# Seven products instead of eight for the down-projection of three SwiGLUs

## The chip, the cores and the metric

The kernel runs on one core of a Trainium2 chip. The metric is the device time of one execution in microseconds (us). A core has five engines with a queue of instructions each, worked off in order: TensorE (PE: products of matrices, with the weight loads PEld beside them), VectorE (DVE), ScalarE (ACT), GpSimd (POOL) and SyncE (SP), which here only issues transfers. POOL also issues transfers, among them those that add to what stands at the destination. The engines work at the same time and wait for one another by semaphores.

## The reference

The reference is a decoder trunk of two layers on 512 tokens of 1024 float32 features. Each layer is SwiGLU, mixer (windowed attention and a short convolution side by side), SwiGLU:

```
x = x + 0.5 * swiglu(rms_norm(x), wg, wu, wd)     # SwiGLU 1 and 3
x = x + concat([attention, conv]) @ w_out         # mixer
x = x + 0.5 * swiglu(rms_norm(x), wg, wu, wd)     # SwiGLU 2 and 4
swiglu(h) = (silu(h @ wg) * (h @ wu)) @ wd        # wg, wu: 1024 x 2816, wd: 2816 x 1024
```

A last norm ends it. The change concerns `@ wd` in SwiGLUs 2, 3 and 4.

## The kernel before

The kernel keeps float32 accuracy with the faster fp32r products: each operand is split into a high part (a cast on ScalarE, line 190) and a low part (a subtraction on VectorE, line 191), and a product is the sum of three parts, high by high, high by low and low by high. So each tile of weight costs a load, a cast, a subtraction, and then its products.

x lies transposed in eight tiles `xs` of 128 features by 512 tokens. The 2816 inner features of a SwiGLU are 11 blocks of 256. A list of stages orders the work: `FIRST` for SwiGLU 1, `INNER` for 2 and 3, `LAST` for 4. ("p", b) is the up-projection of one block in plain form, ("w", b) that of the two blocks b and b+1, and ("d", blocks) the down-projection of these blocks, in which `down` yields 8 output chunks and line 810 adds half of each to x.

A ("w", b) stage (`winograd2`, products at line 725) computes gate and up with seven products of quarter matrices instead of eight, after Winograd's form of Strassen's method. `CHAINS` lists the seven: the accumulator (x, y or w in PSUM), the operand made from the normed activations (b11, b21, t2, t3, t1, t4, b22), and whether it starts anew. The weight quarters a11, a12, s2, s3, s1, a22, s4 come from `FORMS`. `up2` plans their transfers in two halves h each: s1 and s3 are sums that a second, accumulating transfer from POOL makes in the buffer (line 185), s2 and s4 are sums on VectorE (lines 208 and 234). The operands are made by `Norm.make` ahead of use, from the normed activations in `full`.

The weight tiles go through three stations. `need_raw` issues loads on SP into 8 buffers `raw`, `need_split` makes high and low parts into 3 buffers each (`wh`, `wl`), two tiles ahead of the products, and `take_split` hands them over. The activations of a w stage are transposed on TensorE (line 771, `turn`), split and stored as high and low parts in buffers of `g4` (8 of them). `flush` runs the pending transposes within the stages that follow. In the last SwiGLU, `Finale` (lines 827 to 945) computes the last four block pairs with tokens on the partitions, adds x, norms and stores.

The program is recorded line by line, and a scheduler then sets the order on each engine by data and buffers; the semaphores follow from that order.

Of the kernel before, what the change touches and what calls it, by code (L numbers as in the profile page):

```python
# [15 lines left out]
P = 128  # L16
# [13 lines left out]

FIRST = (
# [24 lines left out]
def trunk_kernel(  # L56
# [38 lines left out]
    def g4(name, dt=F32R, shape=(P, 2, S)):  # L95
        return work.tile(list(shape), dt, tag="g4", bufs=8, name=name)
# [96 lines left out]
    def need_split(g):  # L193
        while state["split"] <= min(g, len(order) - 1):
# [6 lines left out]
            elif isinstance(what, tuple):  # L201

                what, h, far = what
                last = {"a11": 0, "a12": 4, "s2": 2, "s3": 6, "s1": 2, "a22": 8, "s4": 4}[what]
                need_raw(u + max(last, 4) + h + LOAD_AHEAD)
                a11, s1, a12, s3, a22 = (raw_of.get(u + 2 * i + h) for i in range(5))
                if what == "s2":
                    nc.vector.tensor_add(a11, a11, s1)
                raw = {"a11": a11, "a12": a12, "s2": a11, "s3": s3, "s1": s1, "a22": a22, "s4": a12}[what]
            else:  # L210

                need_raw(u + 4 + LOAD_AHEAD)
                a11, a12, s1, s3, a22 = (raw_of.get(u + i) for i in range(5))
                if what == "s2":
                    nc.vector.tensor_add(a11, a11, s1)
                if what == "s4":
                    nc.vector.tensor_add(a11, a11, a12)
                raw = {"a11": a11, "a12": a12, "s2": a11, "s3": s3, "s1": s1, "a22": a22, "s4": a11}[what]
                if what == FORMS[-1]:
                    for i in range(5):  # L220
                        del raw_of[u + i]
# [60 lines left out]
    def plan():  # L282
# [20 lines left out]
        def up2(wg, wu, b, far):  # L303
            def at(w, half, h):
                return w, KC // 2 * half + 2 * h, 2, 2 * b * P, S

            u = len(units)
            for what in (
                ((wg, 0),), ((wu, 0), (wu, 1)), ((wg, 1),), ((wu, 0), (wg, 0)), ((wu, 1),)
            ):  # L310
                for h in range(2):
                    add_unit(*(at(w, half, h) for w, half in what))
            order.extend(
                (u, (what, h, far and what == "a11" and h == 0)) for what in FORMS for h in range(2)
            )

        def ffn(wg, wu, wd, stages):
            for what, b in stages:
# [5 lines left out]
                if what == "w":  # L324
                    up2(wg, wu, b, b == 1)
# [24 lines left out]
    xs = [xpool.tile([P, S], F32, tag=f"x{c}", name=f"x{c}") for c in range(KC)]  # L350
# [10 lines left out]
    class Norm:  # L361
# [60 lines left out]
        def scale(self, room):  # L422

            self.full = [g4(f"hf_{self.i}_{n}", F32, (P, 2, S)) for n in range(KC // 2)]
            for c in range(KC):
                nc.vector.scalar_tensor_tensor(
                    self.full[c // 2][:, c % 2, :],
# [6 lines left out]
            self.forms = {}  # L434
            self.sums = [room(f"sum{n}_{self.i}", F32, (P, KC // 2, H)) for n in range(2)]

        def make(self, *names):


            for what in names:  # L440
                hi, lo = (form(f"f{what}{n}_{self.i}") for n in "hl")
                self.forms[what] = (hi, lo)
                for q in range(2):
                    at = slice(2 * q, 2 * q + 2)
                    b11, b12, b21, b22 = (
                        self.full[2 * j + q][:, :, t * H : (t + 1) * H]
                        for j in range(2)
                        for t in range(2)
                    )
                    t3, t2 = (t[:, at, :] for t in self.sums)  # L450
                    if what == "t2":
                        nc.vector.tensor_sub(t3, b12, b22)
                        nc.vector.tensor_sub(t2, t3, b11)
                    if what == "t1":
                        nc.vector.tensor_sub(b12, b11, b12)
                    if what == "t4":
                        nc.vector.tensor_add(t2, t2, b21)
                    src = {"b11": b11, "b21": b21, "b22": b22, "t1": b12, "t3": t3}.get(what, t2)
                    split(hi[:, at, :], lo[:, at, :], src)
# [6 lines left out]
    xin = [g4(f"xin_{n}", F32) for n in range(4)]  # L466
# [130 lines left out]
    def ffn(norm, stages, after=None, late=None):  # L597
# [4 lines left out]
        def plain(b):  # L602
# [9 lines left out]
            hi, lo = g4(f"ah_{norm.i}_{b}"), g4(f"al_{norm.i}_{b}")  # L612
# [6 lines left out]
            if norm.inv is None:  # L619
# [3 lines left out]
                norm.scale(stock if first else g4)  # L623
# [17 lines left out]
        def winograd(b):  # L641
# [10 lines left out]
            hi, lo = g4(f"ah_{name}"), g4(f"al_{name}")  # L652
# [44 lines left out]
        def winograd2(b, between=None):  # L697
# [12 lines left out]
            for step, (acc, operand, start) in enumerate(CHAINS):  # L710
                if operand not in norm.forms:
                    norm.make(operand)
# [44 lines left out]
                if step == 2:  # L757
                    flush(2, "mm")
                if between:
                    between(step)  # L760
                if not first and step < 3:
                    ahead = CHAINS[step + 4][1]
                    if ahead not in norm.forms:
                        norm.make(ahead)
            for j in range(2):
                acts[b + j] = (g4(f"ah_{name}_{j}"), g4(f"al_{name}_{j}"))

            def turn(c, tag="sc"):
                tp = psum(tag, [P, S], f"at_{name}_{c}")
                for t in range(NT):  # L770
                    nc.tensor.transpose(  # L771
                        tp[:, t * P : (t + 1) * P], ups[t][:, c * P : (c + 1) * P], ident
                    )
                hi, lo = acts[b + c // 2]
# [3 lines left out]

        pending = []
# [6 lines left out]
        end = None  # L786
        for i, (what, b) in enumerate(stages):
            if what == "w":
                if after is None and b == 9:
                    end = Finale()  # L790
                winograd2(b, end and end.step)
# [10 lines left out]
            if final and end:  # L802
                end.down(b, acts, flush)
# [17 lines left out]
    class Finale:  # L821
# [8 lines left out]
        def step(self, n):  # L830

            for at in (0, 1) if n == 0 else (n + 1,):
                t, half = divmod(at, 2)
                if half == 0:
                    self.y.append(form(f"ytok{t}", F32, (P, D)))
                tp = psum("mm", [P, S], f"yt_{t}_{half}")
                for j in range(NT):
                    nc.tensor.transpose(
                        tp[:, j * P : (j + 1) * P],
                        xs[half * NT + j][:, t * P : (t + 1) * P],  # L840
                        ident,
                    )
                nc.scalar.copy(self.y[t][:, half * S : (half + 1) * S], tp)

        def widen(self, half, i, pairs):
            if half == 0:
                _, hi, lo = take_split()
            else:
                u = len(units) - pairs + i
                need_raw(u)  # L850
                hi, lo = (form(f"ww{n}_{i}", shape=(P, 2, S)) for n in "hl")
                split(hi, lo, raw_of.pop(u))
            self.w[half].extend((hi[:, k, :], lo[:, k, :]) for k in range(2))

        def products(self, acc, rhs, half, t, c0, a, b):

            tok = slice(t * P, (t + 1) * P)
            cols = slice(c0, c0 + acc.shape[1])
            for k in range(a, b):
                ah, al = rhs[k]  # L860
# [3 lines left out]
                nc.tensor.matmul(  # L864
                    acc, al[:, tok], wh[:, cols], start=False, stop=k + 1 == self.blocks
                )
# [19 lines left out]
        def down(self, blocks, acts, flush):  # L886
# [7 lines left out]
            pairs = len(blocks)  # L894
            self.blocks = 2 * pairs
            rhs = []

            def take(blocks):
                rhs.extend((acts[k][0][:, j, :], acts[k][1][:, j, :]) for k in blocks for j in range(2))


            ready = blocks[:-2]
            take(ready)
            for i in range(len(ready)):
                self.widen(0, i, pairs)
            accs = [psum("mm", [P, S], f"end_0_{t}") for t in range(NT)]
            for t in range(NT):
                self.products(accs[t], rhs, 0, t, 0, 0, len(rhs))
                flush()
            take(blocks[-2:])  # L910
            for i in range(len(ready), pairs):
                self.widen(0, i, pairs)
            for t in range(NT):
                rest = done[:, t : t + 1]
                self.products(accs[t], rhs, 0, t, 0, 2 * len(ready), len(rhs))
                self.close(accs[t], 0, t, 0, rest)
                nc.vector.tensor_scalar(rest, rest, 1.0 / D, EPS, op0=ALU.mult, op1=ALU.add)
                if t == 0:
                    for i in range(pairs):
                        self.widen(1, i, pairs)  # L920
            for t in range(NT):
# [4 lines left out]
                for i in range(steps):  # L926
                    ssq = small(f"ssq_end{t}_{i}", 1)
                    acc = psum("mm", [P, wide], f"end_1_{t}_{i}")
                    self.products(acc, rhs, 1, t, i * wide, 0, len(rhs))
# [18 lines left out]
    def mix(l, norm, after):  # L948
# [23 lines left out]
        for g in range(NKV):  # L972
            h = g4(f"mh_{l}_{g}"), g4(f"ml_{l}_{g}")
# [124 lines left out]
        for pair in range(2):  # L1098
# [21 lines left out]
            hi, lo = g4(f"mh_{l}_{2 + pair}"), g4(f"ml_{l}_{2 + pair}")  # L1120
# [59 lines left out]
```

## Time and profile before

| | |
|---|---|
| three runs | 1723.38, 1723.80, 1723.99 us; median 1723.8 |
| profiled execution | 1723.67 us, span 1721.9 us from the first to the last instruction |
| busy: TensorE, weight loads, VectorE, ScalarE, POOL | 1713.1, 1418.3, 1229.7, 844.2, 156.6 us |
| granted clock of TensorE | 1.0 |
| moved by DMA | 237.85 MB, 138 GB/s in the mean |

The page of the profile gives busy times for each engine, and groups instructions by line and tile. The chain of waits follows the work back from the last instruction, each step to what released it; shares of that chain say which engine sets the time. A row of a timeline or of the chain in order of time has the start, the length in us, the engine, the line and the operation; "x24" merges 24 equal neighbours. The view of stretches gives the busy time of each engine in a part of the span. The end of a matmul is modelled, so successive starts are the better measure of its cost.

### The profile page before, as it was taken

What the parts mean: (1) busy time and instruction counts of PE and PEld (TensorE: products, weight loads), DVE (VectorE), ACT (ScalarE), POOL (GpSimd) and SP (SyncE); (2) the same over time, 40 slices, a digit from 0 to 9 for tenths busy, and PEclk for the clock granted to TensorE, in tenths of its full rate; (3) what the DMA queues carried; (4) which work ended last, traced back from release to release, by engine and by line L of the source; (5) the groups of instructions that cost most, each with busy time, mean ns of one, the idle gap of its engine ahead of it and who ended that gap; (6) DMA issues with size and microseconds to landing.
All of it is one profiled execution on the core that took longest, in us unless ns stands there. A gap on an engine that the chain in (4) does not pass through costs nothing.

```text
span 1721.9 us, 20808 instructions
## 1 busy us (share of the span) xinstructions
PE 1713.1 (99%) x7922; PEld 1418.3 (82%) x7922; DVE 1229.7 (71%) x1694; ACT 844.2 (49%) x1227; POOL 156.6 (9%) x142
## 2 busy tenths in 40 slices
PE   9999999999999999999999999999999999999998
PEld 7888888988888888888888888888888888888887
DVE  7986666678858866766698666666787598666763
ACT  6544444456545544444465444444565465354353
POOL 1011000001201110110011100100022011100101
PEclk9999999999999999999999999999999999999999
DMA  8467455421337674574366745743124458664541
GB/s 245 107 164 208 132 135 150 128 78 58 105 108 146 172 199 131 135 195 132 102 147 179 203 131 136 184 145 99 51 62 123 117 115 221 159 178 125 138 135 49
DMA packets 201207, 237.85 MB, mean 138 GB/s; under 512 B 7628, under 2 KB 125460, under 8 KB 201108
## 3 DMA queue, kind: packets, MB, share of 16 engines
q1 hardware_dynamic: 176932, 189.46, 35.9%
q0 software_dynamic: 23024, 45.62, 16.0%
q8 instruction: 62, 1.02, 0.2%
q10 hardware_dynamic: 1152, 1.45, 0.2%
q14 instruction: 37, 0.30, 0.1%
HBM read 229.68 MB, written 2.10 MB: 135 GB/s over the span
## 4 chain that ended last, share of the span: by engine, by line
PE 97%; DVE 2%; ACT 1%; issue 0%; ACTq 0%; DVEq 0%
PE x L725 24%; PE acc L256 15%; PE acc L259 15%; PE acc L263 15%; PE y L725 12%; PE w L725 6%; PE at L771 2%; PE end L864 1%; PE end L862 1%; PE end L863 1%; PE x L669 1%; PE pt L1048 1%; DVE p L1041 0%; DVE wl L191 0%; ACT p L1033 0%; PE y L669 0%
## 5 line engine op out<-in xcount | busy, mean ns | idle before, releaser
L190 ACT CAST wh<-raw 128x1024 fp32r<-128x1024 f32 (+2 forms) x424 | 443.0, 1045 | 616.1 <-PE acc L259 243.1
L191 DVE TENSOR_TENSOR wl<-raw,wh 128x1024 fp32r<-128x1024 f32 (+2 forms) x423 | 518.5, 1227 | 232.7 <-ACT wh L190 231.5
L256 PE MATMUL acc<-ah,wh 128*128 128x512 f32 x640 | 254.4, 399 | 0.2 <-ACT ah L190 0.2
L263 PE MATMUL acc<-ah,wl 128*128 128x512 f32 x640 | 250.0, 391 | 0.0
L259 PE MATMUL acc<-al,wh 128*128 128x512 f32 x640 | 249.1, 389 | 0.0
L810 DVE SCALAR_TENSOR_TENSOR x<-acc,x 128x512 f32<-128x512 f32 x176 | 119.8, 689 | 107.0 <-PE acc L263 106.4
L256 PE MATMUL acc<-xh,wh 128*128 128x512 f32 x448 | 176.6, 394 | 0.1
L259 PE MATMUL acc<-xl,wh 128*128 128x512 f32 x448 | 175.2, 391 | 0.1
L263 PE MATMUL acc<-xh,wl 128*128 128x512 f32 x416 | 162.4, 390 | 0.0
L263 PEld LDWEIGHTS acc<-ah,wl 128*128 128x128 f32 x640 | 120.1, 188 | 26.0
L256 PEld LDWEIGHTS acc<-ah,wh 128*128 128x128 f32 x640 | 120.0, 188 | 24.0 <-ACT ah L190 1.4
L259 PEld LDWEIGHTS acc<-al,wh 128*128 128x128 f32 x640 | 120.4, 188 | 23.3
L185 POOL DMA_DIRECT2D raw<-in_ffn_wu_dram x39 | 47.2, 1211 | 807.9 <-DVE u L749 394.0
L259 PEld LDWEIGHTS acc<-xl,wh 128*128 128x128 f32 x448 | 84.2, 188 | 18.1 <-DVE xl L377 1.5
L256 PEld LDWEIGHTS acc<-xh,wh 128*128 128x128 f32 x448 | 84.2, 188 | 17.6 <-ACT xh L376 0.5
L263 PEld LDWEIGHTS acc<-xh,wl 128*128 128x128 f32 x416 | 78.1, 188 | 16.4
L190 ACT CAST ah<-at 128x512 fp32r<-128x512 f32 x76 | 44.0, 584 | 67.7 <-PE at L771 67.6
L185 POOL DMA_DIRECT2D raw<-in_ffn_wg_dram x39 | 47.1, 1208 | 236.2 <-DMA raw<-in_ffn_wu_dram 110.1
L191 DVE TENSOR_TENSOR al<-at,ah 128x512 fp32r<-128x512 f32 x76 | 51.9, 687 | 14.9 <-ACT ah L190 14.7
L725 PE MATMUL w<-wh,fb21h 128*128 128x512 f32 x152 | 59.5, 392 | 0.0
L725 PE MATMUL x<-wh,ft2h 128*128 128x512 f32 x152 | 59.5, 392 | 0.0
L725 PE MATMUL y<-wh,ft3h 128*128 128x512 f32 x152 | 59.5, 391 | 0.0
(297 smaller groups left out, 3415.1 us busy)
## 6 DMA issues: line engine op xcount, KB each, us to landing
raw<-in_ffn_wu_dram SPq DMA_DIRECT2D x127, 512.0 KB, 3.7
raw<-in_ffn_wg_dram SPq DMA_DIRECT2D x87, 512.0 KB, 4.7
raw<-in_ffn_wd_dram SPq DMA_DIRECT2D x82, 512.0 KB, 3.4
raw<-in_ffn_wu_dram POOLq DMA_DIRECT2D x39, 512.0 KB, 7.6
raw<-in_ffn_wg_dram POOLq DMA_DIRECT2D x39, 512.0 KB, 6.0
raw<-in_w_in_dram SPq DMA_DIRECT2D x36, 512.0 KB, 3.6
raw<-in_w_out_dram SPq DMA_DIRECT2D x16, 512.0 KB, 4.1
wl<-raw POOLq DMA_DIRECT2D x9, 512.0 KB, 5.3
```

The lines of the kernel that those rows point to most:

```text
L185: nc.gpsimd.dma_start(out=r, in_=rows_of(*more), accum_op=ALU.add)
L190: nc.scalar.copy(hi, raw)
L191: eng.tensor_sub(lo, raw, f32(hi))
L256: nc.tensor.matmul(acc, hi[:, k, :], rhs[k][0], start=k == 0, stop=False)
L259: nc.tensor.matmul(acc, hi[:, k, :], rhs[k][1], start=False, stop=n == 0 and k == last)
L263: nc.tensor.matmul(acc, lo[:, k, :], rhs[k][0], start=False, stop=k == last)
L669: nc.tensor.matmul(out, w[:, k, cols], x_[:, k, :], start=start and k + i == 0, stop=k == KC // 2 - 1 and i == 2, skip_group_check=not start,)
L725: nc.tensor.matmul(out, x_[:, 2 * h + k, tok], w[:, k, :], start=start and h + k + i == 0, stop=h + k == 2 and i == 2, skip_group_check=no ...
L771: nc.tensor.transpose(tp[:, t * P : (t + 1) * P], ups[t][:, c * P : (c + 1) * P], ident)
L810: nc.vector.scalar_tensor_tensor(xs[c], acc, 0.5, xs[c], op0=ALU.mult, op1=ALU.add)
L862: nc.tensor.matmul(acc, ah[:, tok], wh[:, cols], start=k == 0, stop=False)
L863: nc.tensor.matmul(acc, ah[:, tok], wl[:, cols], start=False, stop=False)
```

## The change

`INNER` and `LAST` lose the down-projections of blocks 1 to 8 between the w stages. The five w stages follow one another, then come two stages ("s", 1) and ("s", 5), each the down-projection of four blocks (1024 features) with seven products of quarter matrices, and then ("d", (9, 10)) as before. In the new function `share` the weight block stands and 256 tokens of an operand stream; each product's accumulator is added to the quarter of x it belongs to, with its sign (`SHARES`). The activations of the eight blocks are stored unsplit in float32 (`raws`, copied by ScalarE); a class `Seven`, taken out of `Norm`, makes the operands for both uses, in one operation of 1024 columns where there were two of 512. The weight of the down-projection is planned by the same function as gate and up (`seven`, formerly `up2`); its sum of a12 and the summed a11 is made by an accumulating transfer of POOL inside SBUF instead of by VectorE. The buffers `g4` become half as many `g8` of double size, and the x tiles lie in pairs. `Finale` keeps only blocks 9 and 10; its transposes of x move from stage ("w", 9) into its own first half.

```diff
 INNER = (
-    ("p", 0), ("d", (0,)), ("w", 1), ("w", 3), ("d", (1, 2)), ("w", 5), ("d", (3, 4)), ("w", 7),
-    ("d", (5, 6)), ("w", 9), ("d", (7, 8)), ("d", (9, 10)),
+    ("p", 0), ("d", (0,)), ("w", 1), ("w", 3), ("w", 5), ("w", 7), ("w", 9), ("s", 1), ("s", 5),
+    ("d", (9, 10)),
 )
-LAST = INNER[:-2] + (("d", (7, 8, 9, 10)),)
+LAST = INNER[:-1] + (("d", (9, 10)),)
+SHARES = ((0, 0, 1), (0, 0, 1), (1, 0, -1), (1, 1, 1), (1, 1, -1), (1, 0, 1), (0, 1, 1))
...
-    def g4(name, dt=F32R, shape=(P, 2, S)):
-        return work.tile(list(shape), dt, tag="g4", bufs=8, name=name)
+    def g8(name, dt=F32R, shape=(P, 2, 2, S)):
+        return work.tile(list(shape), dt, tag="g8", bufs=4, name=name)
...
-                if what == "s3":
+                if what == "s3" and how == "share":
+                    nc.gpsimd.dma_start(out=a12, in_=a11, accum_op=ALU.add)
+                elif what == "s3":
                     nc.vector.tensor_add(a12, a12, a11)
...
+                if what == "s":
+                    seven(
+                        lambda o, j, h: (wd, 2 * b + KC // 2 * j + 2 * h, 2, o * S, S),
+                        lambda what, h: "share",
+                    )
...
+            elif b < 9:
+                raws[b] = g8(f"raw_a_{name}", F32, (P, KC // 2, S))
...
+                if b in raws:
+                    nc.scalar.copy(raws[b][:, c, :], tp)
+                    return
...
+        def share(b, ops, between):
+            accs = {}
+            for step, (acc, operand, start) in enumerate(CHAINS):
+                ops.make(operand)
+                xh, xl = ops.forms[operand]
+                if start:
+                    tag = {"x": "mm", "y": "sc", "w": "aux"}[acc]
+                    accs[acc] = [psum(tag, [P, 2, H], f"{acc}_{ops.name}_{m}") for m in range(2)]
+                o, t, sign = SHARES[step]
+                for h in range(2):
+                    _, wh, wl = take_split()
+                    for c in range(4):
+                        out = accs[acc][c // 2]
+                        cols = slice(c * P, (c + 1) * P)
+                        for k in range(2):
+                            parts = ((wh, xh), (wh, xl), (wl, xh))
+                            for i, (w, x_) in enumerate(parts):
+                                nc.tensor.matmul(
+                                    out[:, c % 2, :],
+                                    w[:, k, cols],
+                                    x_[:, 2 * h + k, :],
...
+                                )
+                        if h and c % 2:
+                            part = xpair[2 * o + c // 2][:, :, t * H : (t + 1) * H]
+                            nc.vector.scalar_tensor_tensor(
+                                part, out, 0.5 * sign, part, op0=ALU.mult, op1=ALU.add
+                            )
+                if step < 3:
+                    ops.make(CHAINS[step + 4][1])
+                between(step)
...
+            if what == "w" and b == 9:
+                ops = shared(1)
+                winograd2(b, lambda step: step > 2 and ops.make(CHAINS[step - 3][1]))
+            elif what == "w":
+                winograd2(b)
+            if what == "s" and b == 1:
+                then = shared(5)
+                share(b, ops, lambda step: step > 2 and then.make(CHAINS[step - 3][1]))
+            elif what == "s":
+                share(b, then, lambda step: 2 <= step < 6 and flush(1, "aux"))
```

More of the change, by code (lines that the diff above doesn't have):

```diff
@@ L442, in make @@
                 self.forms[what] = (hi, lo)
[L443 to L459, printed above, removed]
+                b11, b12, b21, b22 = (
+                    self.full[j][:, :, t * H : (t + 1) * H] for j in range(2) for t in range(2)
+                )
@@ L462, in trunk_kernel, with room_g8, room_stock, room_form @@
+                if src is None:
+                    src = self.sums[0 if what == "t3" else 1]
+                split(hi, lo, src)
+    def room_g8(name):
+        t = g8(f"sums_{name}", F32, (P, 2, KC // 2, H))
+        return t[:, 0], t[:, 1]
+    def room_stock(name):
+        return [stock(f"sum{n}_{name}", shape=(P, KC // 2, H)) for n in range(2)]
+    def room_form(name):
+        return [form(f"sum{n}_{name}", F32) for n in range(2)]
     norm = Norm(0)
@@ L710, in winograd2 @@
             for step, (acc, operand, start) in enumerate(CHAINS):
-                if operand not in norm.forms:
-                    norm.make(operand)
+                norm.make(operand)
                 xh, xl = norm.forms[operand]
@@ L758, in winograd2 @@
                     flush(2, "mm")
+                if not first and step < 3:
+                    norm.make(CHAINS[step + 4][1])
                 if between:
                     between(step)
[L761 to L766, printed above, removed]
+            if first:
+                for j in range(2):
+                    acts[b + j] = parts_of(f"a_{name}_{j}")
+            elif b < 9:
+                raws[b] = g8(f"raw_a_{name}", F32, (P, KC // 2, S))
             def turn(c, tag="sc"):
@@ L801, in ffn @@
             final = i + 1 == len(stages)
-            if final and end:
-                end.down(b, acts, flush)
+            if final and after is None:
+                Finale().down(rhs)
                 return
@@ L845, in widen, with turn @@
[L845 to L855, printed above, removed]
+        def turn(self, t, half):
+            if half == 0:
+                self.y.append(form(f"ytok{t}", F32, (P, D)))
+            tp = psum("sc", [P, S], f"yt_{t}_{half}")
+            for j in range(NT):
+                nc.tensor.transpose(
+                    tp[:, j * P : (j + 1) * P],
+                    xs[half * NT + j][:, t * P : (t + 1) * P],
+                    ident,
+                )
+            nc.scalar.copy(self.y[t][:, half * S : (half + 1) * S], tp)
@@ new lines, in widen, with products @@
+        def widen(self, half, pairs):
+            for i in range(pairs):
+                if half == 0:
+                    _, hi, lo = take_split()
+                else:
+                    u = len(units) - pairs + i
+                    need_raw(u)
+                    hi, lo = (form(f"ww{n}_{i}", shape=(P, 2, S)) for n in "hl")
+                    split(hi, lo, raw_of.pop(u))
+                self.w[half].extend((hi[:, k, :], lo[:, k, :]) for k in range(2))
+        def products(self, rhs, half, t, c0, wide):
+            acc = psum("mm", [P, wide], f"end_{half}_{t}_{c0}")
@@ L972, in mix @@
         for g in range(NKV):
[L973 removed]
+            h = parts_of(f"m_{l}_{g}")
             amix[g] = h
```

131 lines of the change are left out of this document (62 added, 69 removed).

## The prediction

> **What bounds the kernel now.** I read the page first, then the chain of work that ended last, then the chain in order of time, and last the order in which the instructions of the two built programs stand on each engine.
>
> ```profile
> span 1721.9 us, 20808 instructions
> PE 1713.1 (99%) x7922; PEld 1418.3 (82%) x7922; DVE 1229.7 (71%) x1694; ACT 844.2 (49%) x1227; POOL 156.6 (9%) x142
> GB/s 245 107 164 208 132 135 150 128 78 58 105 108 146 172 199 131 135 195 132 102 147 179 203 131 136 184 145 99 51 62 123 117 115 221 159 178 125 138 135 49
> PE 97%; DVE 2%; ACT 1%; issue 0%; ACTq 0%; DVEq 0%
> ```
>
> TensorE (PE) carries 97% of the chain and is without work for 9 us of the span. So every product taken away is worth its full spacing, as long as the other engines deliver. A busy PE is no peak, because matmuls overlap; the price of a product is the distance from one start to the next.
>
> ```profile
> 67.40 5.44 PE x L725 x24
> 303.66 2.87 PE x L669 x24
> 306.54 2.88 PE w L669 x24
> 299.42 0.39 PE L256 MATMUL acc<-ah,wh 128*128 128x512 f32 x1
> 303.05 0.39 PE L259 MATMUL acc<-al,wh 128*128 128x512 f32 x1
> ```
>
> In the chain, 24 products of 512 columns take 5.44 us, 226.7 ns each (L725). The down-projection's products have the same spacing: from 299.42 to 303.05 there are 16, 226.9 ns each. The 24 products of 256 columns at L669, block 10 of the first SwiGLU, take 2.88 us, 120 ns each. Half of 226.7 would be 113.3, so a product of half the width costs 6.7 ns more than half. L669 has the form that the new products have: a 128x128 block of the weight stands, 256 tokens stream, and the three parts are high by high, high by low, low by high, each with its own weight load.
>
> **The change part by part: TensorE.** Eight blocks of 256 features in the down-projection are 16 slices of 128 by 8 output chunks by 3 parts, 384 products of 512 columns, in each of SwiGLUs 2 to 4. The new groups are 2 x 7 products of quarter matrices, each 4 slices by 4 chunks by 3 parts: 672 products of 256 columns. The order of the built programs agrees: over the kernel 1140 products of 512 columns and 24 of 256 go, and 2016 of 256 come (the last SwiGLU had some of its old ones in halves). By the spacings above: -1140 x 0.2267 = -258.4 us, +1992 x 0.120 = +239.0 us, together **-19.4 us**, 6.4 per SwiGLU. The transposes stay in number and only move: those of block pair 9 (L771) go beside the second group, those of `Finale` from block pair 9 into its first half.
>
> The Trainium skill, "TensorE: Matmul & The Clock Gate", sections on the issue gap and on LDWEIGHTS, speaks against narrow products: a weight load takes its columns / 1.2, 107 ns, a product N / 2.4 + 2.5, 109 ns at N = 256, and both set the spacing. Wholly overlapped that would be 109 ns, in series 216. The trace's 120 ns lies near the first and decides.
>
> **VectorE (DVE).** What rises is its work. Each of the 28 weight quarters per SwiGLU is split (16 tiles before), 14 operand forms are made from the float32 activations (14 splits and 8 sums or differences), and x is updated 28 times instead of 32.
>
> ```profile
> L191 DVE TENSOR_TENSOR wl<-raw,wh 128x1024 fp32r<-128x1024 f32 x413 | 509.9, 1237 | 227.1 <-ACT wh L190 225.9 <-issue 0.5 <-PE yt L838 0.2
> L810 DVE SCALAR_TENSOR_TENSOR x<-acc,x 128x512 f32<-128x512 f32 x176 | 119.8, 689 | 107.0 <-PE acc L263 106.4
> 575.29 3.49 DVE L191 TENSOR_TENSOR wl<-raw,wh 128x1024 fp32r<-128x1024 f32 x3
> 553.91 1.88 DVE L810 SCALAR_TENSOR_TENSOR x<-acc,x 128x512 f32<-128x512 f32 x3
> ```
>
> A split lasts 1237 ns in the mean and an update of x 689 ns, but back to back they overlap. Three splits take 3.49 us, so with 1.22 for the last one the spacing is (3.49 - 1.22) / 2 = 1.135 us; three updates give (1.88 - 0.68) / 2 = 0.60. In the new order of VectorE, from the first split of the first group to the first split of the second, stand 14 splits, 11 forms or sums for forms, 2 weight sums and 14 operations of 512 columns: 27 x 1.135 + 14 x 0.60 = 39.0 us, against 14 x 48 / 2 = 336 products x 0.120 = 40.3 us of TensorE. In block pair 9, which makes the first forms ahead, it is 26 x 1.135 + 10 x 0.60 = 35.5 us against 168 x 0.2267 + 16 transposes, 39.8 us. In the second group it is 19 x 1.135 + 17 x 0.60 = 31.8 us. So VectorE fits, at 97% in the first group. The price of being this full is bounded by these stages:
>
> ```profile
> 545.00:554.00 9.00, 8.78 (x39) 6.97 (x38) 8.84 (x15) 3.84 (x7) 0.89 (x1) 1.00 0.86 173
> 554.00:592.00 38.00, 38.00 (x169) 31.23 (x168) 34.39 (x40) 22.74 (x29) 3.60 (x3) 1.00 0.64 165
> 592.00:632.00 40.00, 40.00 (x186) 33.20 (x185) 29.66 (x33) 22.17 (x28) 4.67 (x4) 1.00 0.69 180
> ```
>
> The columns are the stretch, PE, PEld, DVE, ACT, POOL busy, then clock, DMA share and GB/s. From 545 to 554 VectorE is busy for 8.84 of 9 us and TensorE loses 0.22; from 554 to 592, at 34.39 of 38, it loses nothing. The low end is 0, by the second row. The high end takes the mean durations in place of the spacings: 27 x 1.237 + 14 x 0.689 = 43.0 us, 2.7 more than TensorE's 40.3, 8 us for three SwiGLUs. I take 40.3 / 9 x 0.22 = 1.0 per SwiGLU, **+3 us**, because the first row is the nearest in load. The splits run two quarters ahead of the products, so a lag under about one quarter (24 x 0.120 = 2.9 us) is swallowed; beyond it the next quarter's low part is late and TensorE waits. Behind an update of x, which waits for TensorE, stand on VectorE the splits of the next two quarters.
>
> **ScalarE, POOL and the queues.**
>
> ```profile
> L190 ACT CAST wh<-raw x424: 407/1055/1063, 5.4 to 1680.7; 128x1024 fp32r<-128x1024 f32 x138, 128x768 fp32r<-128x768 f32 x3, 128x256 fp32r<-128x256 f32 x1
> L185 POOL DMA_DIRECT2D raw<-in_ffn_wu_dram x39: 1194/1203/1332, 32.6 to 1602.3; - x39
> L229 POOL DMA_DIRECT2D wl<-raw x9: 852/889/904, 534.1 to 1393.7; - x9
> DMA to landing us min/median/max: 5.6/6.1/11.6
> DMA to landing us min/median/max: 4.4/5.3/9.2
> raw<-in_ffn_wd_dram SPq DMA_DIRECT2D x82, 512.0 KB, 3.4
> 590.14 1.23 DVE L208 TENSOR_TENSOR raw<-raw,raw 128x1024 f32<-128x1024 f32 x1
> 594.56 1.23 DVE L208 TENSOR_TENSOR raw<-raw,raw 128x1024 f32<-128x1024 f32 x1 [1.45 <-DMA raw<-in_ffn_wu_dram]
> ```
>
> ScalarE casts 14 quarters and 7 forms per group, 21 x 1.055 = 22 us of 40.3: hidden under TensorE, cost 0. Per SwiGLU SP issues 20 loads for the eight blocks instead of 16; POOL issues 8 accumulating loads (L185's kind, 1.2 us each) and 4 sums of a12 and a11 inside SBUF (L229's kind, 0.9 us): 13 us over two groups of 40, on an engine that is 9% busy. An accumulating load lands after 6.1 us, at worst 11.6 (the first landing row), a sum in SBUF after 5.3, at worst 9.2 (the second), a plain load after 3.4. In the new order a buffer of the weight stream is freed six to eight quarters before its next content is split, 6 x 2.88 = 17 us or more, against 3.4 + 11.6 = 15 us at worst where a load and an accumulation follow each other, and those have eight quarters. What queues behind the sum in SBUF is the load of a22 on SP and all loads after it; a22 has 17 us for 9.2 + 3.4. Where two up-projections already follow each other, the second weight sum waited 1.45 us for its accumulation at 594.56, and TensorE did not stop (40.00 of 40). After the change such junctions occur five more times per SwiGLU. Cost: 0, with the high end in the slow rival.
>
> **The end.** `Finale` then holds two block pairs, not four.
>
> ```profile
> 1700.37 1.28 ACT L881 ACT_TABLE_LOAD   x1
> 1704.28 0.69 DVE L872 SCALAR_TENSOR_TENSOR ytok<-end,ytok 128x512 f32<-128x512 f32 x1 [0.95 <-PE end L864]
> 1707.48 0.36 ACTq L945 DMA_DIRECT2D out_dram<-ytok  x1
> ```
>
> In its second half TensorE gives a token tile every 12 x 0.2267 = 2.72 us instead of 5.44. From the sum to the issue of the store one tile takes 1707.48 - 1704.28 = 3.2 us, and the first has a table load of 1.28 before it. The chain falls behind by up to 1.28 + 3 x (3.2 - 2.72) = 2.7 us; the engines work on neighbouring tiles in between, so the low end is 0. I take **+1 us**.
>
> Forms of 1024 columns in place of two of 512 (1.135 against 2 x 0.60 us) save VectorE about 1 us per SwiGLU ahead of the groups; TensorE does not wait there, so it counts 0. The pairs of buffers (g8 for g4) keep the number of bytes, and in the built order the first SwiGLU and the mixers keep their sequence on TensorE: 0.
>
> **The sum.** The profiled execution took 1723.67 us, span 1721.9 and 1.8 around it, 0.1 from the median 1723.8. 1723.67 - 19.4 + 3 + 1 = **1708.3 us**.
>
> **The rivals.**
> - *VectorE becomes the bound in the first group.* For it: 97% by spacings, over 100% by mean durations, and each wait of the in-order engine comes on top. Against it: the lead of two quarters, and the second group, in which it has 8 us to spare. Price: the 8 us above in place of 3, and some waiting at the junctions: 1713.3, with an upper end near 1718.
> - *The weight stream starves the groups (slower).* A group moves 14 quarter loads and 2 sums of 512 KB, 16 x 0.524 = 8.4 MB, in 40.3 us: 208 GB/s. The densest stage of this kind in the trace, two up-projections in a row, moved 180 GB/s (592 to 632). Were 180 the ceiling, a group would take 46.6 us, +6.3, six times: +38, 1746 us. It decides when a group takes (1723.7 - 1708.3) / 6 = 2.6 us longer, at 196 GB/s. For it: accumulating transfers land late (11.6). Against it: slices of 43 us at 245, 221 and 208 GB/s, a DMA share of only 0.69 at 180, and TensorE at 100% there.
> - *The weight load shows through at 256 columns.* The Trainium skill's page on TensorE has both operations set the spacing, as said above. A mechanism of this kernel would be that a load cannot run under the product before it. By the rows a load lasts 188 ns:
>
> ```profile
> L263 PEld LDWEIGHTS acc<-ah,wl 128*128 128x128 f32 x640 | 120.1, 188 | 26.0
> ```
>
>   Spaced at 188 the new products would cost 1992 x 0.068 = 135 us more, 1844. L669 held 120 ns over 168 products in a row, with the same operands; this is nearly excluded.
>
> **How the numbers follow.** The forecast with its own range, 1703 (no waits, no tail) to 1711.5, gets 0.61. VectorE's bound (1711.5 to 1718) gets 0.20. The starved stream gets 0.11, the weight load 0.01. The rest, 0.07, is a wait at a buffer that I did not see: 0.02 still faster, 0.03 near the old time, 0.02 beyond. The range 1703 to 1718 takes in the first two, 0.81; I set the upper end to 1719 for the junctions. About 0.2%, 3.4 us, is what a measurement of this kernel tells from no change: faster 0.83, same 0.03, slower 0.14.
>
> **What would show it.** In the profile after, 24 of the new products stand at 2.88 us in the chain, with the page's PE near 1694 us and its share at 99%. If VectorE binds, TensorE's idle time stands ahead of the new products with the low weight parts (`wl`) as releaser, in the first group of each SwiGLU and not in the second. If the stream binds, VectorE or ScalarE waits for `raw` with DMA as releaser and both groups stretch. The tail shows as the distance from the last product to the last store. The prediction is wrong if the groups take much over 40.3 us each, or if an order of buffers makes block pairs 3 to 9, now without a down-projection between them, wait for their loads.

## The result, and the profile after

The changed kernel takes 1704.0 us (1703.7 to 1704.7) against 1723.7 for the kernel before: a ratio of 0.989, 95% interval 0.987 to 0.990, or -19.7 us. The forecast was 1708.3, with a range from 1703 to 1719. The profiled execution took 1704.74 us, with a span of 1703.0. The page of the kernel after:

```profile
span 1703.0 us, 22763 instructions
PE 1692.1 (99%) x8774; PEld 1443.3 (85%) x8774; DVE 1312.4 (77%) x1712; ACT 916.5 (54%) x1277; POOL 196.7 (12%) x178
PE 94%; DVE 3%; DMA 1%; ACT 1%; issue 0%; SPq 0%; ACTq 0%; DVEq 0%
```

VectorE (DVE) gained 83 us of work, ScalarE 72 and POOL 40, and TensorE (PE) lost 21. TensorE still has work in 99% of the span. What TensorE waited for, as the view of waits lists it (total us, times, longest):

```profile
PE idle L125 <- DVE warm L518: 1.2, 1, 1.2
PE xt L536 <- DMA xin<-in_x_dram: 1.2, 1, 1.2
PE o L1127 <- DVE pl L1116: 0.8, 2, 0.4
PE x L756 <- DMA wl<-raw: 0.4, 1, 0.4
```

None of these lies in the new groups: the first two are the start of the kernel, the third is the mixer, the fourth (at 890.39 us) the first w stage of SwiGLU 3. The chain in order of time, in SwiGLU 2:

```profile
752.03 5.75 PE x_s L836 x48
757.79 5.76 PE w_s L836 x48
...
786.59 11.52 PE x_s L836 x96
...
828.62 5.75 PE x_s L836 x48
```

48 products of 256 columns take 5.76 us, 120 ns each, from the first step to the last: the price that the prediction took from block 10 of SwiGLU 1. The stretches that answer to those of before (the first and second row), and then the last up-projection stage, the first group and the second group of SwiGLU 2 (columns as before):

```profile
545.00:554.00 9.00, 9.00 (x41) 7.17 (x39) 8.80 (x12) 3.44 (x5) 2.05 (x2) 1.00 0.82 172
592.00:632.00 40.00, 40.00 (x185) 32.96 (x184) 27.89 (x29) 22.12 (x28) 6.03 (x5) 1.00 0.74 188
712.19:752.03 39.84, 39.84 (x186) 33.09 (x185) 36.45 (x37) 27.57 (x35) 3.84 (x4) 1.00 0.73 185
752.03:792.35 40.32, 40.32 (x339) 40.32 (x338) 39.84 (x43) 22.01 (x23) 6.32 (x7) 1.00 0.85 209
792.35:834.37 42.02, 42.02 (x353) 42.02 (x353) 32.64 (x37) 17.62 (x20) 3.75 (x4) 1.00 0.74 189
```

The fourth row is the one to look at. In the first group VectorE is busy for 39.84 of 40.32 us, the weight loads all the time, the DMA share is 0.85 at 209 GB/s, and TensorE loses nothing. All three of the rivals' resources are close to full here at the same time, and none of them shows as a wait. So there were two questions for the experiments: whether the gain is the products' alone, and how near to its end this stage stands.

### The profile page after: what moved, and what is told of

It is laid out like the page before. It is cut to its first block, busy times and chain, and to the rows that moved or that the text cites. A ratio compares the mean times of both kernels' runs of the same rounds, so it can differ in the third digit from the quotient of the medians.

```text
span 1703.0 us, 22763 instructions
## 1 busy us (share of the span) xinstructions
PE 1692.1 (99%) x8774; PEld 1443.3 (85%) x8774; DVE 1312.4 (77%) x1712; ACT 916.5 (54%) x1277; POOL 196.7 (12%) x178
## 4 chain that ended last, share of the span: by engine, by line
PE 94%; DVE 3%; DMA 1%; ACT 1%; issue 0%; SPq 0%; ACTq 0%; DVEq 0%
PE x L756 24%; PE y L756 12%; PE acc L267 10%; PE acc L270 10%; PE acc L274 10%; PE x_s L836 8%; PE w L756 6%; PE y_s L836 4%; PE w_s L836 2%; PE at L803 2%; DMA wl<-raw 1%; PE x L701 1%; PE pt L1112 1%; DVE p L1105 0%; PE end L946 0%; PE end L945 0%
## 5 line engine op out<-in xcount | busy, mean ns | idle before, releaser
L198 ACT CAST wh<-raw 128x1024 fp32r<-128x1024 f32 (+2 forms) x462 | 482.6, 1045 | 581.3 <-PE x L756 136.5
L199 DVE TENSOR_TENSOR wl<-raw,wh 128x1024 fp32r<-128x1024 f32 (+2 forms) x461 | 564.0, 1225 | 222.6 <-ACT wh L198 220.8
L270 PE MATMUL acc<-a,wh 128*128 128x512 f32 x224 | 87.4, 390 | 0.0
L267 PE MATMUL acc<-a,wh 128*128 128x512 f32 x224 | 87.2, 398 | 0.0
L274 PE MATMUL acc<-a,wl 128*128 128x512 f32 x224 | 87.0, 391 | 0.0
L893 DVE SCALAR_TENSOR_TENSOR x<-acc,x 128x512 f32<-128x512 f32 x88 | 59.0, 685 | 32.0 <-PE acc L274 31.8
L217 DVE TENSOR_TENSOR raw<-raw,raw 128x1024 f32<-128x1024 f32 x50 | 60.6, 1219 | 3.1 <-DMA raw<-in_ffn_wu_dram 2.2
L756 PE MATMUL x<-wl,fb11h 128*128 128x512 f32 x152 | 59.5, 391 | 0.5 <-DMA wl<-raw 0.4
L756 PE MATMUL w<-wl,fb21h 128*128 128x512 f32 x152 | 59.5, 391 | 0.0
L756 PE MATMUL x<-wl,ft2h 128*128 128x512 f32 x152 | 59.3, 390 | 0.0
L756 PE MATMUL w<-wh,fb21l 128*128 128x512 f32 x152 | 59.2, 390 | 0.0
```

What stands on the lines that cost most here:

```text
L198: nc.scalar.copy(hi, raw)
L199: eng.tensor_sub(lo, raw, f32(hi))
L267: nc.tensor.matmul(acc, hi[:, k, :], rhs[k][0], start=k == 0, stop=False)
L270: nc.tensor.matmul(acc, hi[:, k, :], rhs[k][1], start=False, stop=n == 0 and k == last)
L274: nc.tensor.matmul(acc, lo[:, k, :], rhs[k][0], start=False, stop=k == last)
L756: nc.tensor.matmul(out, x_[:, 2 * h + k, tok], w[:, k, :], start=start and h + k + i == 0, stop=h + k == 2 and i == 2, skip_group_check=no ...
```

## The experiments

**Is the gain the products'?** The theory is that the whole gain is the TensorE term. The rival is that part of it comes from what came along: whole-width forms, paired buffers, the new end. In the first run the stage lists and the last part are those of the kernel before, and what does not belong to the groups themselves is kept; in the next two, one SwiGLU has the groups.

```diff
+INNER_OLD = (
+    ("p", 0), ("d", (0,)), ("w", 1), ("w", 3), ("d", (1, 2)), ("w", 5), ("d", (3, 4)), ("w", 7),
+    ("d", (5, 6)), ("w", 9), ("d", (7, 8)), ("d", (9, 10)),
+)
+LAST_OLD = INNER_OLD[:-2] + (("d", (7, 8, 9, 10)),)
+STAGES = (FIRST, INNER_OLD, INNER_OLD, LAST_OLD)  # side_parts
+STAGES = (FIRST, INNER, INNER_OLD, LAST_OLD)      # only_2
+STAGES = (FIRST, INNER_OLD, INNER_OLD, LAST)      # only_4
```

> The changed kernel with the stage lists of the kernel before: plain eight-product down-projections and the old last part, but all the side parts kept (whole-width forms, residual in pairs of blocks, the larger buffers). Theory 'the gain is the products': no difference, 1723.7 us within 0.2%. Rival 'the side parts carry a share of the gain': 1710 to 1720 us.

> Only SwiGLU 2 has its two groups of seven products; SwiGLUs 3 and 4 are as in the kernel before. Theory: one third of the TensorE term, -6.5 us, 1717.3 us. Rival 'the gain comes from the end of the kernel or from one SwiGLU': no difference, 1723.7 us.

> Only SwiGLU 4 has its two groups of seven products and the new last part; SwiGLUs 2 and 3 are as in the kernel before. Theory: -6.5 us for the products and 0 to +1 us for the end, 1717.2 to 1718.2 us. Rival 'the new last part carries the gain': well below that, 1710 us or less.

Measured: 1723.45 us with the side parts alone, ratio 1.0001 (0.9992 to 1.0009), so they are worth nothing that this run can tell. With SwiGLU 2 alone it is 1716.9, ratio 0.9962 (0.9949 to 0.9974), -6.8 us; with SwiGLU 4 alone 1717.7, 0.9966 (0.9954 to 0.9979), -6.0. No run has SwiGLU 3 alone; what remains for it of 19.7 is 6.9. The pages of the first two runs differ in the work of TensorE alone by the amount of the gain:

```profile
PE 1712.7 (99%) x7922; PEld 1417.8 (82%) x7922; DVE 1227.1 (71%) x1650; ACT 841.3 (49%) x1199; POOL 156.8 (9%) x142
```

```profile
PE 1706.1 (99%) x8210; PEld 1426.9 (83%) x8210; DVE 1253.9 (73%) x1668; ACT 866.5 (51%) x1225; POOL 169.8 (10%) x154
```

TensorE lost 6.6 us of work from the first to the second, although it has 288 more products; VectorE and ScalarE gained 27 and 25 us, and these cost nothing. The gain is the products', in SwiGLUs 2 and 4 by these runs and in SwiGLU 3 by the difference, and SwiGLU 4 gives back some 0.8 at the end.

**What does half the width cost?** The kernel before, with the same arithmetic, but every product of the down-projections outside `Finale` in two halves:

```diff
         if own:
+            for t in range(2):
+                at = slice(t * H, (t + 1) * H)
+                for k in range(last + 1):
+                    for i, (w, x_) in enumerate(((hi, rhs[k][0]), (hi, rhs[k][1]), (lo, rhs[k][0]))):
+                        nc.tensor.matmul(
+                            acc[:, at], w[:, k, :], x_[:, at],
+                            start=t == 0 and k + i == 0, stop=k == last and i == 2,
+                            skip_group_check=True,
+                        )
```

> The kernel before, with each of the 1,920 products of 512 columns in its down-projections made as two of 256 columns; the same arithmetic. Theory 'a product of 256 columns takes 0.120 us on the path': 1920 x (0.240 - 0.2267) = +25.5 us, 1749 us. Rival 'the 192 ns weight load shows through as soon as the products are narrow': 1920 x (0.384 - 0.2267) = +302 us, 2026 us.

Measured: 1750.6 us, ratio 1.0158 (1.0144 to 1.0171), +26.9. The chain and the waits of this run:

```profile
290.11 2.87 PE acc L258 x24
296.73 11.51 PE acc L258 x96
```

```profile
PE acc L258 <- ACT ah L190: 3.3, 3, 1.3
```

The halves keep 120 ns over 96 products (11.51 / 96), although each has its own weight load. The run is 1.4 us above the forecast. TensorE waits 3.1 us longer than before for activations (3.3 against 0.2), in three places, the down-projection of block 0 in SwiGLUs 2 to 4, which is more than that difference; by the spacings alone the halves thus cost somewhat less than the sum. The rival with the weight load falls: it would have added 302 us.

**How near is VectorE to its end?** Three runs add work to VectorE in the groups: the two weight sums that the change gave to a transfer (2.3 us in each group), four repeated subtractions (4.5 us), and seven (7.9 us).

```diff
-                if what == "s3" and how == "share":                                  # sum_vector
-                    nc.gpsimd.dma_start(out=a12, in_=a11, accum_op=ALU.add)
-                elif what == "s3":
+                if what == "s3":
                     nc.vector.tensor_add(a12, a12, a11)
...
                 split(hi, lo, raw)                                                   # vector_more
+                if isinstance(order[n][1], tuple) and how == "share" and h == 0:
+                    nc.vector.tensor_sub(lo, raw, f32(hi))
...
+                if isinstance(order[n][1], tuple) and how == "share" and h == 0 and what in FORMS[:4]:  # vector_four
+                    nc.vector.tensor_sub(lo, raw, f32(hi))
```

> The changed kernel, with the weights' sum for the seventh form of the groups made by VectorE (two additions of 1.14 us in each group) instead of an accumulating transfer. Theory 'VectorE has a lead': in the first group it writes each low part 2.8 to 3.4 us before TensorE takes it, so 2.3 us more are covered, 1704.0 us within 0.7 us. Rival 'VectorE is at its bound in the first group, 98.8% busy': +2.3 us in each of three first groups, 1711 us.

> The changed kernel, with the low part of every other weight form of the groups made twice on VectorE: seven more subtractions of 1.14 us in each group, the results the same. Theory 'a lead of 3 us, then every microsecond shows': in the first group VectorE needs about 47.7 us against TensorE's 40.3, 7.4 less 3 of lead are +4 to +4.6 us; in the second 40.5 against 42.0, nothing; for three SwiGLUs +12 to +14 us, 1717 us. Rival 'the busy share overstates VectorE, and there is room': 1704 us. Rival 'no lead at all': 6 x 7.9, up to +48 us, 1752 us.

> As the run with seven more subtractions in each group, but with four: 4.5 us more for VectorE in each group. Theory 'VectorE's two-quarter lead is the margin': between the 2.3 us that cost nothing and the 7.9 us that cost 9 us for a SwiGLU lies the lead of about 3 us, so 4.5 us cost some 0 to 1.5 us for a SwiGLU: 1704 to 1708.5 us. Rival 'the loss is proportional to the added work': 4/7 of 27 us, 1719.5 us.

Measured: 1703.8 us with 2.3 us more, the same as without; 1715.5 (ratio to the kernel before 0.9955, 0.9941 to 0.9968) with 4.5, +11.4 or 3.8 for a SwiGLU; 1731.2 (1.0042, 1.0027 to 1.0057) with 7.9, +27.2 or 9.1 for a SwiGLU. So the theory of a lead holds for the first 2.3 us, and it was too generous beyond: it allowed 4.5 at the most for four subtractions, and 14 for seven. The rivals miss as well: a loss proportional to the added work was 15.5 us for four subtractions, VectorE at its bound was 2.3 in each of three first groups for the sums, and for seven it was to be either nothing or up to 48. The two groups of SwiGLU 2 in the run with the sums on VectorE:

```profile
752.19:792.50 40.31, 40.31 (x338) 40.31 (x338) 39.80 (x43) 20.79 (x22) 4.83 (x5) 1.00 0.71 184
792.50:834.50 42.00, 42.00 (x352) 41.91 (x352) 36.72 (x41) 18.59 (x21) 1.36 (x2) 1.00 0.61 164
```

VectorE shows 43 operations in the first group and 39.80 us, as the changed kernel does (43 in 39.84), although two of them are new; the second group has 41 where the changed kernel has 37: two sums of its own and two operations that the first group no longer took over. So a busy share of 99% does not say that VectorE is late. It works ahead into the next group while it can, and stays busy either way. The waits of the run with four and, in the second fence, with seven subtractions:

```profile
PE x_s L838 <- DVE wl L242: 3.5, 3, 1.2
PE y_s L838 <- DVE wl L242: 2.1, 3, 0.7
PE y_s L838 <- ACT wh L198: 2.1, 3, 0.7
```

```profile
PE w_s L838 <- DVE wl L242: 5.9, 3, 2.0
PE y_s L838 <- DVE wl L242: 4.6, 6, 0.8
PE x_s L838 <- DVE wl L242: 2.3, 3, 1.7
PE y_s L838 <- ACT wh L198: 1.9, 3, 0.7
```

These are 7.7 and 14.7 us, where 11.4 and 27.2 were lost. One part of the rest is seen in stretches of 2 us, in the second group of SwiGLU 2, with seven subtractions:

```profile
808.00:810.00 2.00, 0.77 (x5) 0.53 (x4) 2.00 (x3) 0.67 (x1) 0.00 (x0) 1.00 1.01 197
810.00:812.00 2.00, 0.84 (x4) 0.84 (x5) 2.00 (x3) 0.00 (x0) 0.00 (x0) 0.65 1.14 225
812.00:814.00 2.00, 2.00 (x11) 2.00 (x11) 2.00 (x3) 0.00 (x0) 0.00 (x0) 0.50 0.20 37
814.00:816.00 2.00, 2.00 (x19) 2.00 (x19) 0.57 (x1) 0.97 (x2) 0.00 (x0) 1.00 0.58 177
```

After two stalls within 4 us the granted clock falls to 0.50, and 11 products stand where 19 did: a stall is paid again, in slower products behind it. Such a fall lasts 3.41 us, of which up to half, 1.7 us, is lost; it comes once in each SwiGLU with seven subtractions (5.1 us at most) and in SwiGLU 4 alone with four (1.7 us). Another part is not listed as a wait: a wait counts from the modelled end of the product before it, 0.28 us after its start, where the next product was due after 0.12. At 0.16 us for each of 9 and 15 waits that is, as an estimate, 1.4 and 2.4 us. What then remains, some 0.6 and 5 us, is not traced.

Most of the stalls with seven subtractions stand in the second group, where the expectation had VectorE 1.5 us faster than TensorE. VectorE is late there: TensorE begins the group with five of the seven forms still to make, t2 to b22 (first fence). In the changed kernel, whose second group begins at 792, t2, t3 and t1 are done by then, t1 as the last (second fence):

```profile
793.64 0.28 PE L838 MATMUL x_s<-fb11h_s,wh 128*128 128x256 f32 x1
795.01 1.22 DVE L199 TENSOR_TENSOR ft2l_s<-sum_s,ft2h_s 128x1024 fp32r<-128x1024 f32 x1
...
820.72 1.22 DVE L199 TENSOR_TENSOR fb22l_s<-raw_a,fb22h_s 128x1024 fp32r<-128x1024 f32 x1
```

```profile
787.23 1.22 DVE L199 TENSOR_TENSOR ft1l_s<-raw_a,ft1h_s 128x1024 fp32r<-128x1024 f32 x1
```

So the steps that failed in these two expectations are that the second group costs nothing and that a stall costs its own length. How the loss divides between the two groups is not separated here.

**Is the weight stream near its end?** Four of the sixteen quarter loads of each group are sent twice.

```diff
                 load(r, n, 0, kc)
+                if n in twice:
+                    load(r, n, 0, kc)
...
                 if what == "s":
+                    twice.update(len(units) + 2 * i for i in (0, 1, 2, 4))
```

> The changed kernel, with four of the sixteen quarter loads of each group sent twice: 2.1 MB more in each group. Theory 'the stream has room up to a DMA share of 1': share .85 becomes 1.06 in the first group, which is 2.5 us too much, less the lead of the buffers; 0 to +2.5 us for each SwiGLU, 1704 to 1712 us. Rival 'the stream is already at its limit at about 209 GB/s': 2.1 MB / 209 GB/s = 10 us in each of six groups, +60 us, 1764 us.

Measured: 1721.6 us, scattered from 1711 to 1726; ratio to the kernel before 0.9983 (0.9968 to 0.9998), +17.6 against the changed kernel. It fits neither: too much for room up to a share of 1, far too little for a limit at 209 GB/s. The waits, the chain and two stretches:

```profile
PE w_s L840 <- ACT wh L201: 10.2, 3, 5.4
PE w_s L840 <- DVE wl L202: 2.2, 4, 0.8
```

```profile
784.57 6.11 DMA raw<-in_ffn_wd_dram
790.69 8.38 DMA raw<-in_ffn_wd_dram
```

```profile
782.00:792.00 10.00, 10.00 (x86) 10.00 (x85) 10.00 (x11) 5.98 (x6) 2.42 (x2) 1.00 0.91 283
792.00:802.00 10.00, 7.00 (x57) 6.59 (x56) 2.83 (x4) 1.99 (x2) 0.92 (x1) 1.00 0.92 248
```

At 283 GB/s over 10 us the stream has no limit at 180 or 209. What stops TensorE is one late quarter for each SwiGLU: its two transfers land one after the other, 6.11 and then 8.38 us, as the chain shows; both write the same buffer, and SyncE issues the second when the first has landed. The granted clock fell behind the late quarters too (to 0.50 from 802.51 us for 3.41 us, and from 1645.61 for 6.83). So the run shows a cost of lateness, not a limit of rate, and a clean answer on the rate it is not.

**A version that follows from it.** If a product of 512 columns costs 226.7 ns and two of 256 cost 240, the groups of SwiGLU 4 can gain by wide products: its result is wanted with tokens on the partitions anyway. x is turned in place during the up-projections, and the groups then hold the tokens and stream 512 weight columns.

```diff
+        def share_tokens(b, ops, between):
...
+                                nc.tensor.matmul(
+                                    out,
+                                    x_[:, 2 * h + k, tok],
+                                    w[:, k, :],
...
+                            y = xs[NT * o + 2 * t + u]
+                            nc.vector.scalar_tensor_tensor(y, out, 0.5 * sign, y, op0=ALU.mult, op1=ALU.add)
...
+        def to_tokens(half):
+            tps = [psum(tag, [P, S], f"yt_{half}_{t}") for t, tag in enumerate(("mm", "mm", "aux", "aux"))]
...
-                self.turn(at % NT, at // NT)
```

> The changed kernel, with the residual of SwiGLU 4 turned to tokens on the partitions before its two groups (in place, in the stages of the activations), so that the groups' products keep the tokens stationary and stream 512 weight columns: 24 products of 0.2267 us in a step instead of 48 of 0.120 us. Theory 'width is worth what the rows say': 14 steps x (5.76 - 5.44) = -4.5 us against the changed kernel, 1699.5 us. Rival 'another limit of the groups takes over': 1704 us.

Measured: 1699.0 us, ratio to the kernel before 0.9854 (0.984 to 0.9869): -5.0 against the changed kernel, where -4.5 was expected. The chain has the new price, 24 products in 5.44 us:

```profile
1590.20 5.44 PE x_s L871 x24
1595.64 5.44 PE w_s L871 x24
```

On top of this, one group of seven products went into SwiGLU 1, for its blocks 2 to 5.

```diff
 FIRST = (
-    ("p", 0), ("p", 1), ("d", (0,)), ("w", 2), ("d", (1,)), ("w", 4), ("d", (2, 3)), ("w", 6),
-    ("d", (4, 5)), ("w", 8), ("d", (6, 7)), ("u", 10), ("d", (8, 9, 10)),
+    ("p", 0), ("p", 1), ("d", (0,)), ("w", 2), ("d", (1,)), ("w", 4), ("u", 10), ("w", 6),
+    ("d", (10,)), ("w", 8), ("s", 2), ("d", (6, 7)), ("d", (8, 9)),
 )
```

> The kernel with tokens on the partitions in SwiGLU 4, and in SwiGLU 1 blocks 2 to 5 of the down-projection as one group of seven products as well (block 10 of the up-projection goes before the last two pairs, its down-projection alone). Theory: 192 x 0.2267 = 43.5 us of products go and 336 x 0.120 = 40.3 come, -3.2 us; the single SwiGLUs measured -6.8 for two groups, so up to -3.4: 1695.6 to 1695.8 us. Rival 'the first SwiGLU has a stage that this order starves': 1699 us or more.

Measured: 1696.6 us (1695.9 to 1697.4), ratio to the kernel before 0.9841 (0.9828 to 0.9855), -27.2. The step itself is -2.4 by the medians, 0.8 short of the -3.2 expected; the spans of the profiled executions (1697.3 and 1694.1) differ by 3.2, but the second is the fastest execution of its kernel. TensorE's work fell from 1688.0 to 1683.6 us. This is the fastest version of this study.

## Why the prediction was right, and where it was not

- **TensorE, -19.4 us: right.** The spacing of 120 ns held (5.76 us for 48, and 11.51 for 96 in the run with halves), and one SwiGLU is worth 6.8 (SwiGLU 2) and 6.9 (SwiGLU 3, by the difference) where 6.4 was forecast. The excess of some 0.4 for a SwiGLU is not traced further. On the rule of the Trainium skill, "TensorE: Matmul & The Clock Gate", in its sections on the issue gap and on LDWEIGHTS: the trace agrees that both overlap, at 120 ns where an estimate by the page's figures is 109.
- **VectorE's lag, +3 us: this step failed.** It measured 0. The term was read off the stretch from 545 to 554, where VectorE was busy for 8.84 of 9 us and TensorE lost 0.22. That wait has a name in the timeline of the kernel before (first fence). The second fence has the cast that ended it, and the third the same cast in the kernel after:

```profile
545.58 0.97 PE L256 MATMUL acc<-ah,wh 128*128 128x512 f32 x3 [0.22 <-ACT ah L190]
```

```profile
544.93 0.60 ACT L190 CAST ah<-gate 128x512 fp32r<-128x512 f32 x1
```

```profile
544.57 0.60 ACT L198 CAST a<-gate 128x512 fp32r<-128x512 f32 x1
```

  TensorE waited once, in the down-projection of block 0, for ScalarE's high part of the second slice of activations. VectorE had finished that slice at 543.59, but until 545.02 ScalarE was at two operations on weights that stand ahead of the cast in its order. The changed kernel keeps this stage, ScalarE begins the cast 0.36 us earlier, and TensorE loses nothing, although VectorE is just as full (8.80 of 9 us, the first row of the stretches after). So the wait was ScalarE's order at one junction; it was no price of a full VectorE and should not have been multiplied by 40.3 / 9. The sum by spacings, 39.0 us against 40.3, was the better reading, and the sentence beside it, that a lag under one quarter (2.9 us) is swallowed, agrees with the run that adds 2.3 us at no cost. The upper end of 8 us, by mean durations, did not come near.
- **The end, +1 us: right in size.** `Finale` holds two blocks of 256 features where it had four. From the start of the last product to the end of the span it was 1721.9 - 1715.15 = 6.75 us before, and is 7.42 after:

```profile
1715.15 0.28 PE L864 MATMUL end<-wwh,al 128*128 128x256 f32 x1
```

```profile
1695.58 0.28 PE L946 MATMUL end<-wwh,al 128*128 128x256 f32 x1
...
1699.09 0.34 ACTq L1009 DMA_DIRECT2D out_dram<-ytok  x1
```

  By the two runs with one SwiGLU each it is 0.8 (6.8 less 6.0), if the products of both are worth the same.
- **ScalarE, POOL and the queues, 0: right.** No wait for any of them stands in a group. The junctions of up-projections, five more for a SwiGLU, cost nothing that the waits show; the row from 592 to 632 is at 40.00 of 40. The one wait for a transfer in an up-projection, 0.4 us in SwiGLU 3, follows the down-projection of block 0, which both kernels have.
- **The rivals.** VectorE's bound did not come, but it was close: 2.3 us more for a group are free, 4.5 cost 3.8 us for a SwiGLU. The sign that the prediction gave for it, waits in the first group and not in the second, would have misled: with seven more subtractions most of them stand in the second. The starved stream had its price from a ceiling of 180 GB/s, which was only what that stage had asked for; the first group moved 209 with no wait. The weight load never showed, though it fills the group entirely (40.32 of 40.32).
- **The sum.** 1708.3 was 4.3 us too high: 3 of it are the VectorE term, the rest the excess of the TensorE term and parts of a microsecond elsewhere.

## What to carry to other kernels

Price a stall from the row that names its releaser, not from a stretch in which some engine happens to be full: a full engine that works ahead is not late. Take the path's own unit (the spacing of products) from a stage of the same form and trust it; then ask of the other engines how much more they could bear, by adding work until TensorE waits. Where the two orientations of a product are free to choose, and the data is turned anyway, wide products are worth it; whether they would pay for a turning of their own, no run here shows.

## What the runs showed of the hardware

Stalls of TensorE that sum to about 2 us can cost more than themselves, and whether they do depends on where they lie in time. With four subtractions added, the same pair of waits (0.70 and 1.16 us) stands in the second group of SwiGLUs 2, 3 and 4, but only in SwiGLU 4 does the granted clock fall, to 0.50 for 3.41 us, a loss of 1.7 us of products. With seven, it falls in each of the three, at 810.59, 1148.51 and 1657.10 us: 99 and 149 times 3.413 us lie between. With the loads sent twice, 247 times that lie between the falls at 802.51 and 1645.61. So the falls keep to a grid of 3.41 us within an execution. Stretches on this grid, with four subtractions, counted from the fall at 1650.51, tell the three places apart (the first row is in SwiGLU 2, the second in SwiGLU 3, the last two in SwiGLU 4):

```profile
804.01:807.42 3.41, 2.05 (x16) 1.61 (x14) 3.41 (x4) 1.96 (x2) 1.05 (x2) 1.00 0.86 167
...
1145.34:1148.75 3.41, 2.25 (x18) 2.04 (x19) 3.41 (x5) 0.00 (x0) 0.00 (x0) 1.00 1.05 205
...
1647.10:1650.51 3.41, 1.55 (x11) 1.22 (x10) 3.41 (x5) 0.77 (x1) 0.61 (x1) 1.00 0.99 192
1650.51:1653.92 3.41, 3.41 (x19) 3.41 (x18) 3.41 (x4) 1.20 (x2) 0.00 (x0) 0.50 0.58 115
```

In SwiGLUs 2 and 3 a boundary of the grid divides the pair, and the most that TensorE is idle in one stretch is 1.36 us (3.41 - 2.05). In SwiGLU 4 both waits fall into one stretch, 1.86 us, and the clock is halved at its end. With seven subtractions the stretches before the three falls have 1.82 to 1.97 us idle, and one of 1.67 was followed by none. So the border lies near 1.8 us, about half of a stretch; it is not sharper than that, for with the loads sent twice one stretch of 1.85 us (1137.02 to 1140.43) was followed by no fall.

The Trainium skill, "TensorE: Matmul & The Clock Gate", in its part on the clock gate, has a gate that halves the clock after an idle window of about 3.4 us and watches windows that run freely. The halving, the length and the windows that do not follow the stalls agree with these rows; a whole window without work was not needed, since 1.82 us of idle time were enough.
